# Own buffers and an earlier load for the background matrix-vector blocks of a two-layer trunk

## The chip, the cores and the metric

The kernel runs on one core of a Trainium2 chip. The metric is device time in microseconds (us) of one execution, the median of several runs. The kernel before takes 2971.46 us (three runs, 2971.45 to 2976.05). The core's engines are named as the profile names them: PE (TensorE, with PEld for its weight loads), DVE (VectorE), ACT (ScalarE), POOL (GpSimd) and SP (SyncE, which here only issues DMAs). Each engine takes its own list of instructions in order, and semaphores make it wait for others.

## The reference, cut to what matters

Two layers over 1024 tokens of width 1024, in float32. Each layer has a mixer (gated delta net in layer 0, retention in layer 1) and a convolutional feed-forward. Ahead of each of these the activations are scaled and shifted, and behind it they are gated, by vectors that depend on one conditioning vector `c`:

```python
def reference(x, c, cond_w, cond_b, ada_w, ada_b, ...):
    e = silu(c @ cond_w + cond_b)                       # 1024
    for i in range(2):
        mod = e @ ada_w[i] + ada_b[i]                   # 6 * 1024
        sh1, sc1, g1, sh2, sc2, g2 = split(mod, 6)
        y = mixers[i](x * (1 + sc1) + sh1)
        x = layer_norm(ALPHA * x + (1 + g1) * y, ...)
        y = conv_ffn(x * (1 + sc2) + sh2, ...)
        x = layer_norm(ALPHA * x + (1 + g2) * y, ...)
    return x
```

The product `e @ ada_w[i]` is a matrix-vector product with a 1024 x 6144 matrix. The change is about how ten of the twelve 1024-wide pieces of these products are computed; two of layer 0 are needed at once and are computed in the opening.

## The kernel before

TensorE works in a split float32: each operand is written as a high and a low part, and three matmuls replace one (`mm3`, `mma`). A weight unit is loaded raw into a buffer of tag `wr` (`load_w`, L100; the DMA is L102), ScalarE writes its high part `wh` (L89), VectorE its low part `wl` (L90). The tags `wr`, `wh` and `wl` have two buffers each.

The program runs through these stages: the opening (conditioning vector, the first scales and shifts, the first projections); layer 0's mixer, in which the chunk-by-chunk scan is interleaved with the projections that fill TensorE's gaps (`run`, `scan`, `filler`); its output projection; the first feed-forward, whose up projection is done by Strassen-like products (`strassen`, with one call of `wino` for each pair of weight units) and whose down projection is `proj_gen`; layer 1's projections, again in `strassen`; the retention core, interleaved with the value projections (`core`, `ret_v`, `ret_fill`); its output projection; and the second feed-forward.

A matrix-vector piece is background work. `bg_ada(i, j, kind)` (L205) puts eight functions into a list `bg`: two halves of 512 columns, four blocks each. A block is 256 rows by 512 columns, 512 KB. Its `unit` gets a buffer, issues the load on SP (L214) and returns the arithmetic, `work`: two operations on VectorE (L221, L223), each of which adds one row group, scaled by `e`, to a sum `ada`. There is one buffer of tag `ada`. With the fourth block of a half the sum over the partitions is finished: for a "col" piece by four transposes on TensorE, four accumulating operations on ScalarE (L235) and an addition on VectorE (L237 or L239); for a "row" piece by a matmul with ones (L245) and an addition (L246).

`bg_step` (L119) is called at fixed places of the main work: after each projection unit of the layer 0 mixer, twice in each `wino`, after each weight unit of the retention's value projection, and after each step of `proj_gen`. A call first issues the arithmetic that the last call left in `pend`, then takes the next function from `bg`. So a block's arithmetic is issued one call behind its load. The same list carries `bg_gain` (L377), which multiplies rows by a gain on POOL, with buffers of the tag `lane`.

The block's buffer comes from the ring named in `bg_tag`: `wr`, which the weight loads use as well, and inside `strassen` the ring `lane` (four buffers), which there also holds the two gate tiles `g` of the feed-forward, read by the convolution (L1564). The tag `xT` has four buffers of 128 x 512; the opening takes two of them, and nothing else uses them.

In all 80 blocks are loaded: 24 in the mixer of layer 0, 40 in the first feed-forward (its `strassen` has 40 calls), 8 in the retention core and 8 in the second feed-forward.

The order of the work on each engine is made before the run. TensorE's order in the two interleaved stages is written down by `run` with a clock of estimated latencies (`pq` pins it). All other orders are made by the framework's planner: it takes instructions by priority, earliest in the program first, when its own estimate of times says that their inputs and buffers are there, and it may take a later one when an earlier one isn't ready. On the chip the lists are then followed strictly.

```python
    BUFS = {..., "lane": 4, ..., "ada": 1, "wr": 2, "wh": 2, "wl": 2, ..., "xT": 4}
    ...
    def load_w(src, tags=("wh", "wl"), raw="wr", eng=dve):
        wr = tl(raw, [P, D])
        anchor["w"] = sp.dma_start(wr, src)
```

Of the kernel before, what the change touches and what calls it, by code (L numbers as in the profile page):

```python
# [15 lines left out]
P = 128  # L16
D = 1024
S = 1024
KT = D // P
HALF = 512  # L20
# [13 lines left out]
def trunk_kernel(ctx: ExitStack, tc, A):  # L34
    nc = tc.nc
    pe, act, dve, pool, sp = nc.tensor, nc.scalar, nc.vector, nc.gpsimd, nc.sync
# [4 lines left out]
    dr = ctx.enter_context(tc.tile_pool(name="dr", bufs=1, space=bass.MemoryType.DRAM))  # L41

    BUFS = {"hTa": 8, "hTb": 8, "qkv": 20, "aux": 4, "auh": 8, "lane": 4, "cv": 4, "ada": 1,
            "wr": 2, "wh": 2, "wl": 2, "t2": 3, "sm": 14, "sm2": 6, "st": 8, "s8": 6, "S": 4, "qx": 3, "fs": 1, "xT": 4}

    def tl(tag, shape, dt=F32, name=None):
        return sb.tile(shape, dt, tag=tag, name=name or tag, bufs=BUFS[tag])
# [7 lines left out]
    def ct(name, shape, dt=F32):  # L55
        return cp.tile(shape, dt, tag=name, name=name)
# [25 lines left out]
    def hs(half):  # L82
        return slice(half * HALF, (half + 1) * HALF)
# [30 lines left out]
    bg, pend = [], []  # L114

    bg_ps = [None]
    bg_tag = ["wr"]

    def bg_step(tile=mm_tile):  # L119
        bg_ps[0] = tile  # L120
        if pend:
            pend.pop()()
        if bg:
            nxt = bg.pop(0)()
            if nxt:
                pend.append(nxt)

    def gemm_feat(src, hT_, step=True):
        w = load_w(src)
        accs = [acc_tile() for _ in hT_]  # L130
        for a, ht in zip(accs, hT_):
            for k in range(KT):
                mm3(a, w, k, ht[k], k == 0, k == KT - 1)
        if step:
            bg_step(acc_tile)
        return accs
# [58 lines left out]
    def bias_cols(i, j):  # L195
        return ada_b[:, i * 48 + j * 8:i * 48 + j * 8 + 8]

    def row_load(src, key=None, eng=sp, tag="auh"):
        t = two(tag, F32, "rowb")
        with after(key):  # L200
            for hf in range(2):
                eng.dma_start(t[hf], src[:, hs(hf)].to_broadcast([P, HALF]))
        return t

    def bg_ada(i, j, kind):  # L205
        box = {}

        def unit(nh, kp):
            if kp == 0:
                box["a"] = tl("ada", [P, HALF])  # L210
            a = box["a"]
            wr = tl(bg_tag[0], [P, 2, HALF], name="mvw")
            c0 = j * D + nh * HALF
            sp.dma_start(wr, A["ada_w"][i, kp * 256:(kp + 1) * 256, c0:c0 + HALF].rearrange("(a p) n -> p a n", p=P))  # L214
            return lambda: work(nh, kp, a, wr)

        def work(nh, kp, a, wr):
            for kk in range(2):
                k = kp * 2 + kk
                if k == 0:  # L220
                    dve.tensor_scalar(a, wr[:, 0], e[:, 0:1], None, ALU.mult)  # L221
                else:
                    dve.scalar_tensor_tensor(a, wr[:, kk], e[:, k:k + 1], a, ALU.mult, ALU.add)  # L223
            if kp < KT // 2 - 1:
                return
            if kind == "col":
                if nh == 0:
                    vecs[i, j] = ct(f"v{i}{j}", [P, KT])
                gs = slice(4 * nh, 4 * nh + 4)
                v, b = vecs[i, j][:, gs], bias_cols(i, j)[:, gs]  # L230
                tp, pt = bg_ps[0](), tl("sm2", [P, 4], name="cs")
                for g in range(4):
                    pe.transpose(tp[:, g * P:(g + 1) * P], a[:, g * P:(g + 1) * P], ident)
                for g in range(4):
                    act.activation(a[:, g * P:(g + 1) * P], tp[:, g * P:(g + 1) * P], AF.Copy, accum_out=pt[:, g:g + 1])  # L235
                if j in (1, 2, 4):
                    dve.scalar_tensor_tensor(v, pt, 1.0, b, ALU.add, ALU.add)  # L237
                else:
                    dve.tensor_add(v, pt, b)  # L239
            else:  # L240
                if nh == 0:
                    rows[i, j] = row_load(A["ada_b"][i:i + 1, j * D:(j + 1) * D], ("x", i))
                g = rows[i, j][nh]
                pt = bg_ps[0]()
                pe.matmul(pt, ones, a, start=True, stop=True)  # L245
                dve.scalar_tensor_tensor(g, pt, 1.0, g, ALU.add, ALU.add)  # L246

        for nh in range(2):
            for kp in range(KT // 2):
                bg.append(lambda nh=nh, kp=kp: unit(nh, kp))  # L250
# [126 lines left out]
    def bg_gain(n, src, dst):  # L377
        gb = []

        def unit(c, r):  # L380
            if r == 0:
                gb[:] = [tl("auh", [P, HALF], name="gb") for _ in range(2)]
                for t, nm in zip(gb, ("ln_g", "ln_b")):
                    sp.dma_start(t, A[nm][n:n + 1, hs(c)].to_broadcast([P, HALF]))
            x = tl("lane", [P, HALF], name="xg")
            rs = slice(r * P, r * P + P)
            sp.dma_start(x, src[rs, hs(c)])
            if r == 7:
                return gain(x, rs, c)
            return lambda: gain(x, rs, c)  # L390

        def gain(x, rs, c):
            pool.tensor_tensor(x, x, gb[0], ALU.mult)
            pool.tensor_tensor(x, x, gb[1], ALU.add)
            sp.dma_start(dst[rs, hs(c)], x)

        for c in range(2):
            for r in range(8):
                bg.append(lambda c=c, r=r: unit(c, r))
# [139 lines left out]
    xT = {}  # L539
# [478 lines left out]
    def tail(p, h, q4):  # L1018
# [24 lines left out]
        elif all(("tail", g, 0) in events for g in pairs[p]):  # L1043
            give("lane", 1)
            emit(("M", p))

    bg_ada(0, 4, "col")
    bg_ada(0, 3, "col")
    bg_ada(0, 2, "col")
    kept = {}  # L1050
    zd = dr.tile([GH, P, S], F32, tag="zd", name="zd")
# [50 lines left out]
    c, z = "c", "z"  # L1102
# [54 lines left out]
    def strassen(hT0, xts, scale, shift, items, tags=("hTb", "hTb", "qkv", "qkv", "aux"), direct=False):  # L1157
# [86 lines left out]
            sink(2, prod(a22, "T4"), u3)  # L1244
            bg_step()

        bg_tag[0] = "lane"
        for n in range(2):
            if not direct:
                sinks[n] = items[n][2]()  # L1250
# [9 lines left out]
        for n in range(2, len(items)):  # L1260
            wino(n, items[n][2]())
            if items[n][3]:
                items[n][3]()
        bg_tag[0] = "wr"
        return B

    def ablk_of(src, tag="cv"):
# [247 lines left out]
    def layer_tail(i, mix, wout, xsrc, x_mid, x_out, ln_next, final):  # L1515
# [23 lines left out]
        def pair_items(fp):  # L1539
# [49 lines left out]
            return [(up[4 * fp], up[4 * fp + 2], gate_start, conv), (up[4 * fp + 1], up[4 * fp + 3], up_start, None)]  # L1589

        strassen(hT0, xts, sc2, sh2, [it for fp in range(NF // 2) for it in pair_items(fp)])
        slots = {"c": "hTa", "x": "qkv"}
        gb2 = gain_rows(3, ("mid", i), "hTb") if final else None
# [69 lines left out]
    def gate_item(u):  # L1663
        def start():
            def sink(q, a, b):
# [5 lines left out]

    sc_r, sh_r = next0()
    B = strassen(h0, xts, sc_r, sh_r, [gate_item(0), gate_item(2)]
                 + [rope_item(h, j) for h in range(RH) for j in range(2)] + [gate_item(u) for u in range(4, 16, 2)], ("hTa", "aux", "qkv", "qkv", "hTa"), True)
    hT = [h0, []]
    xlo = []
    for t in range(4):
        x = tl("cv", [P, 516], name="xlo")[:, 0:HALF]
# [270 lines left out]
```

## Time and profile before

| What | us |
|---|---|
| median of three runs | 2971.46 |
| span of the profiled execution | 2967.8 |
| the profiled execution's own time | not given beside its span |
| TensorE busy | 2820.5 (95%) |
| VectorE busy | 2242.4 (76%) |
| ScalarE busy | 1316.5 (44%) |

The span runs from the first to the last instruction of the profiled execution; the runs' times lie some 4 us above it. A row of the groups names the line, the engine, the operation, the tiles (out<-in), the shapes and the count, then busy time, the mean of one in ns, and the idle time of the engine just before it with what ended it. A row of the waits names who waited, for whom, and the total, the number of times and the longest. A row of the timeline has start, length, line, operation and, in brackets, the idle time before it. The chain is followed backwards from the last instruction of a stretch, at each step to what released it. "mvw" is the tile of a background block, `wr` a raw weight unit, `ada` the running sum.

### The profile page before, as it was taken

How to read it: one execution, taken by the hardware profiler on the slowest of the kernel's cores; microseconds unless marked ns; L12 is line 12 of the kernel's file. 1: busy time of each engine (PE TensorE's matmuls, PEld its weight loads, DVE VectorE, ACT ScalarE, POOL GpSimd, SP SyncE). 2: the span in 40 equal slices, each digit the busy share in tenths (PEclk: the TensorE clock that was granted, in tenths of full speed). 3: DMA queues.
4: the chain of work that ended last, by engine and by line, in shares of the span. 5: the costliest groups of instructions: out<-in, count | busy, mean ns of one | idle time of the engine just before them, and what ended most of it. 6: DMA issues, size and time to landing. Idle time of an engine off the chain costs nothing. (4 is left out here: it accounts for less than half of the span.)

```text
span 2967.8 us, 38939 instructions
## 1 busy us (share of the span) xinstructions
PE 2820.5 (95%) x13638; PEld 2304.5 (78%) x13638; DVE 2242.4 (76%) x4005; ACT 1316.5 (44%) x2413; POOL 474.8 (16%) x469
## 2 busy tenths in 40 slices
PE   8999898999999999999999999999999999999997
PEld 7887777887788888787877887777777788887786
DVE  5787787656688888879678645666689887777979
ACT  4744564444544444446433442222344544444443
POOL 0312221100001111610000202322202011112301
PEclk9999999999999999999999999999999999999998
DMA  7231222254245445865333544665664243335753
GB/s 275 79 113 65 86 79 79 83 167 160 91 158 163 158 151 174 305 198 179 120 128 117 181 160 152 203 189 175 205 212 157 91 135 107 107 107 176 274 183 137
DMA packets 244404, 451.01 MB, mean 152 GB/s; under 512 B 23088, under 2 KB 76592, under 8 KB 244208
## 3 DMA queue, kind: packets, MB, share of 16 engines
q1 hardware_dynamic: 213088, 401.07, 41.0%
q10 hardware_dynamic: 29760, 43.00, 4.0%
q0 software_dynamic: 1360, 4.46, 0.4%
q8 instruction: 107, 1.75, 0.3%
q14 instruction: 89, 0.73, 0.1%
HBM read 339.91 MB, written 108.53 MB: 151 GB/s over the span
## 5 line engine op out<-in xcount | busy, mean ns | idle before, releaser
L651 PE MATMUL acc<-hT,wh 128*128 128x512 f32 x960 | 299.3, 393 | 0.0
L1437 PE MATMUL acc<-bb,ab 128*128 128x512 f32 x984 | 231.4, 393 | 6.6 <-DVE bb L90 5.4
L1585 POOL TENSOR_TENSOR o<-o 128x512 f32<-128x512 f32 x80 | 110.7, 1394 | 716.4 <-DVE o L1578 490.8
L1437 PEld LDWEIGHTS acc<-bb,ab 128*128 128x128 f32 x984 | 182.6, 188 | 50.2 <-DVE bb L90 10.2
L1163 PE MATMUL acc<-T,wb 128*128 128x512 f32 x840 | 203.1, 391 | 6.7 <-DVE wb L90 6.7
L651 PEld LDWEIGHTS acc<-hT,wh 128*128 128x128 f32 x960 | 181.9, 190 | 34.1
L651 PE MATMUL acc<-hT,wl 128*128 128x512 f32 x480 | 201.1, 419 | 0.0
L89 ACT ACTIVATE ab<-ar 128x512 fp32r<-128x512 f32 x210 | 129.6, 625 | 152.7 <-PE mm L287 36.9
L90 DVE TENSOR_TENSOR ab<-ar,ab 128x512 fp32r<-128x512 f32 x210 | 161.9, 777 | 41.1 <-ACT ab L89 41.1
L1163 PEld LDWEIGHTS acc<-T,wb 128*128 128x128 f32 x840 | 157.0, 188 | 43.2 <-DVE wb L90 9.8
L90 DVE TENSOR_TENSOR wl<-wr,wh 128x1024 fp32r<-128x1024 f32 x95 | 119.7, 1260 | 69.6 <-ACT wh L89 68.6
L90 DVE TENSOR_TENSOR wb<-mm,wb 128x512 fp32r<-128x512 f32 x216 | 145.5, 682 | 31.2 <-ACT wb L89 30.6
L90 DVE TENSOR_TENSOR wb<-wr,wb 128x512 fp32r<-128x512 f32 x162 | 111.1, 691 | 69.8 <-ACT wb L89 69.1
L89 ACT ACTIVATE wh<-wr 128x1024 fp32r<-128x1024 f32 x95 | 100.7, 1061 | 132.3 <-PE acc L651 53.1
L1224 ACT ACTIVATE pc<-acc 128x512 f32<-128x512 f32 x143 | 84.9, 593 | 160.7 <-PE acc L1163 97.4
L1564 DVE SCALAR_TENSOR_TENSOR o<-g,vc,o 128x512 f32<-128x512 f32 (+2 forms) x176 | 145.4, 843 | 4.7 <-ACT o L1559 4.1
L89 ACT ACTIVATE wb<-mm 128x512 fp32r<-128x512 f32 x216 | 124.0, 595 | 51.9 <-DVE mm L1213 50.3
L89 ACT ACTIVATE wb<-wr 128x512 fp32r<-128x512 f32 x162 | 99.4, 628 | 104.0 <-DMA wr<-in_ffn_up 38.8
L651 PE MATMUL acc<-wh,hT 128*128 128x512 f32 x384 | 135.6, 415 | 1.6 <-DVE vv L90 1.6
L110 PE MATMUL acc<-T,wb 128*128 128x512 f32 x292 | 116.0, 397 | 9.4 <-DVE wb L90 9.4
L472 DVE SCALAR_TENSOR_TENSOR qkv<-raw,vc,qkv 128x512 f32<-128x512 f32 x144 | 111.6, 779 | 11.5 <-ACT qkv L470 10.7
L223 DVE SCALAR_TENSOR_TENSOR ada<-mvw,e,ada 128x512 f32<-128x512 f32 x140 | 106.9, 764 | 17.4 <-DMA mvw<-in_ada_w 17.1
(641 smaller groups left out, 7466.8 us busy)
## 6 DMA issues: line engine op xcount, KB each, us to landing
wr<-in_ffn_up SPq DMA_DIRECT2D x92, 512.0 KB, 4.4
mvw<-in_ada_w SPq DMA_DIRECT2D x80, 512.0 KB, 4.3
ad<-o SPq DMA_DIRECT2D x154, 256.0 KB, 3.1
ar<-ad SPq DMA_DIRECT2D x154, 256.0 KB, 3.9
Br<-in_ffn_down SPq DMA_DIRECT2D x88, 256.0 KB, 3.8
wr<-in_ret_wv SPq DMA_DIRECT2D x32, 512.0 KB, 3.9
ar<-od SPq DMA_DIRECT2D x56, 256.0 KB, 5.3
xs<-xt ACTq DMA_DIRECT2D x24, 512.0 KB, 3.7
```

The source lines that it names most:

```text
L89: act.activation(dst_h, src, AF.Copy)
L90: eng.tensor_tensor(dst_l, src, dst_h, ALU.subtract)
L110: mm(acc, wl[:, k], hl[0], start=first, stop=False)
L223: dve.scalar_tensor_tensor(a, wr[:, kk], e[:, k:k + 1], a, ALU.mult, ALU.add)
L472: dve.scalar_tensor_tensor(oh, raw[:, 3 - j:515 - j], w[:, 3 - j:4 - j], oh, ALU.mult, ALU.add)
L651: pq(pe.matmul(out, lhsT, rhs, start=start, stop=stop), cost)
L1163: return pe.matmul(*a, skip_group_check=True, **kw)
L1224: act.activation(t, X, AF.Copy)
L1437: return pe.matmul(*args, skip_group_check=True, **kw)
L1564: dve.scalar_tensor_tensor(tv, gv[:, c0 - j:c1 - j], w[:, 2 - j:3 - j], tv, ALU.mult, ALU.add)
L1585: (dve if fp == 0 else pool).tensor_tensor(o[d], o[x], o[y], op)
```

## The change

The blocks get buffers of their own: the tag `xT` now has two buffers, each large enough for a block (128 x 2 x 512), in the same space as the four small ones. `bg_tag` goes. A function in `bg` now returns, with its arithmetic, how many calls later that is to be issued: 2 for a block, 1 for a gain. `bg_step` counts these down, in order; once `bg` is empty it issues one left-over arithmetic per call. The sum buffer `ada` is taken at a half's first arithmetic and no longer at its first load.

```diff
-            ..., "fs": 1, "xT": 4}
+            ..., "fs": 1, "xT": 2}
...
-    bg_tag = ["wr"]
...
-        if pend:
-            pend.pop()()
+        for p in pend:
+            p[0] -= 1
+        while pend and (pend[0][0] <= 0 or not bg):
+            pend.pop(0)[1]()
+            if not bg:
+                break
         if bg:
             nxt = bg.pop(0)()
             if nxt:
-                pend.append(nxt)
+                pend.append(list(nxt))
...
         def unit(nh, kp):
+            wr = tl("xT", [P, 2, HALF], name="mvw")
+            c0 = j * D + nh * HALF
+            sp.dma_start(wr, A["ada_w"][i, kp * 256:(kp + 1) * 256, c0:c0 + HALF].rearrange("(a p) n -> p a n", p=P))
+            return 2, lambda: work(nh, kp, wr)
+
+        def work(nh, kp, wr):
             if kp == 0:
                 box["a"] = tl("ada", [P, HALF])
             a = box["a"]
-            wr = tl(bg_tag[0], [P, 2, HALF], name="mvw")
-            c0 = j * D + nh * HALF
-            sp.dma_start(wr, A["ada_w"][i, kp * 256:(kp + 1) * 256, c0:c0 + HALF].rearrange("(a p) n -> p a n", p=P))
-            return lambda: work(nh, kp, a, wr)
-
-        def work(nh, kp, a, wr):
             for kk in range(2):
...
-            return lambda: gain(x, rs, c)
+            return 1, lambda: gain(x, rs, c)
...
-        bg_tag[0] = "lane"
...
-        bg_tag[0] = "wr"
```

More of the change, by code (lines that the diff above doesn't have):

```diff
@@ L43, in trunk_kernel @@
     BUFS = {"hTa": 8, "hTb": 8, "qkv": 20, "aux": 4, "auh": 8, "lane": 4, "cv": 4, "ada": 1,
-            "wr": 2, "wh": 2, "wl": 2, "t2": 3, "sm": 14, "sm2": 6, "st": 8, "s8": 6, "S": 4, "qx": 3, "fs": 1, "xT": 4}
+            "wr": 2, "wh": 2, "wl": 2, "t2": 3, "sm": 14, "sm2": 6, "st": 8, "s8": 6, "S": 4, "qx": 3, "fs": 1, "xT": 2}
     def tl(tag, shape, dt=F32, name=None):
```

## The prediction

> **What bounds the kernel now.** I read the page first, then busy time by stretch, then who waited for whom inside each stretch, then the chain of work that ended last in the one stretch where background blocks are waited for.
>
> ```profile
> span 2967.8 us, 38939 instructions
> PE 2820.5 (95%) x13638; PEld 2304.5 (78%) x13638; DVE 2242.4 (76%) x4005; ACT 1316.5 (44%) x2413; POOL 474.8 (16%) x469
> L223 DVE SCALAR_TENSOR_TENSOR ada<-mvw,e,ada 128x512 f32<-128x512 f32 x140 | 106.9, 764 | 17.4 <-DMA mvw<-in_ada_w 17.1
> ```
> ```profile
> 200.00:560.00 360.00, 331.26 (x2329) 282.02 (x2328) 287.03 (x773) 198.51 (x441) 81.07 (x125) 0.95 0.26 85
> 830.00:1190.00 360.00, 359.60 (x1595) 296.29 (x1594) 310.24 (x485) 173.46 (x339) 50.27 (x36) 1.00 0.48 156
> 1190.00:1230.00 40.00, 33.00 (x137) 25.89 (x136) 34.11 (x42) 16.92 (x38) 26.05 (x17) 0.96 0.92 338
> 1930.00:2030.00 100.00, 92.11 (x402) 68.95 (x400) 64.11 (x119) 20.20 (x34) 20.29 (x28) 0.98 0.62 187
> ```
>
> TensorE bounds it: 95% of the span, so a change helps only where TensorE stands idle. In the second fence each row is a stretch, its length, busy time of PE, PEld, DVE, ACT and POOL, the granted clock, the DMA share and GB/s. The background blocks run in four places: 24 of them under the scan of layer 0 (first row, 28.7 us of idle TensorE), 40 in the first feed-forward (second row, 0.4 us idle), 8 in the retention core (last row, 7.9 us idle), 8 in the second feed-forward. The profiled execution has a span of 2967.8 us; no separate time is given for it, and the median of the runs, 2971.46, is 3.7 us above the span. I add the sum to the median one for one, as the change touches neither end of the program.
>
> ```profile
> PE sc L651 <- DVE Sr L1752: 3.5, 1, 3.5
> PE sc L651 <- DVE on L1780: 1.3, 2, 1.0
> PE acc L651 <- DVE wl L90: 1.0, 2, 0.8
> PE mm L654 <- DVE on L1780: 0.8, 1, 0.8
> PE acc L651 <- DVE vv L90: 0.6, 1, 0.6
> ```
> ```profile
>   DMA mvw<-in_ada_w: 13.6, 6
> ```
> ```profile
> 1951.11 3.82 DMA op<-od
> ...
> 1966.91 4.77 DMA mvw<-in_ada_w
> ...
> 1972.38 1.22 DVE wl L90
> ...
> 1974.26 0.61 DVE Sr L1752
> 1974.91 1.15 PE sc L651 x3
> ...
> 2013.99 4.47 DMA mvw<-in_ada_w
> ```
>
> These are TensorE's waits in 1930:2030 (all five, 7.2 us in total), the idle time of engines before work on mvw in 1900:2060 (13.6 us in six waits), and the chain of 1930:2030. The chain shows how they hang together: VectorE takes its instructions in order, stands before a background block until its load lands (1966.91 + 4.77), then does a weight split, the rest of the block, and only at 1974.26 the state copy Sr for which TensorE waits 3.5 us.
>
> **The change part by part.**
>
> *Loads two calls ahead, retention core.* The block's arithmetic no longer follows its load. If the six waits go, all 7.2 us of TensorE's waits may go. With them goes a slow stretch:
>
> ```profile
> 1968.52 1.52 PE L651 MATMUL sc<-vv,kz 128*128 128x512 f32 x6
> ...
> 1975.86 0.63 PE L651 MATMUL acc<-wh,22_13012 128*128 128x512 f32 x1
> ...
> 1978.85 0.45 PE L651 MATMUL acc<-wl,22_13012 128*128 128x512 f32 x1
> ...
> 1979.37 0.39 PE L651 MATMUL acc<-wh,22_13032 128*128 128x512 f32 x1
> 1979.59 0.40 PE L651 MATMUL acc<-wl,22_13032 128*128 128x512 f32 x1
> ```
>
> Seven matmuls start between 1975.86 and 1978.85, 0.43 us apart; at 1979.37 it is 0.22. Lost: 2.99 - 7 x 0.23 = 1.4 us. Sum for this stage: 7.2 + 1.4 = 8.6 us. Upper bound: the two transfers on the chain, 4.77 + 4.47 = 9.2 us. Lower bound 0: the chain has other transfers of that length ready to be late next (op<-od, 3.82 us), and with two buffers the third and fourth block of each half are still loaded only when the first two are used up, so up to half of the six waits can come back. I take 8.6, as the row nearest to the end, Sr, waits on nothing else late: TensorE's products that it copies (1968.52, six of them) were issued well before the idle time.
>
> *Own buffers, layer 0.* A block no longer takes one of the two wr buffers, so weight loads stop waiting for blocks:
>
> ```profile
> SPq L102 <- DVE ada L223: 52.6, 6, 22.9
> ACT wh L89 <- DMA wr<-in_gdn_wqkv: 14.5, 4, 5.0
> DVE v L239 <- ACT ada L235: 4.0, 1, 4.0
> PE mm L651 <- DVE qkv L928: 6.0, 3, 2.5
> PE mm L654 <- DVE DT L963: 5.8, 3, 2.5
> ```
>
> In 200:560 the SP queue stood 52.6 us before weight loads until blocks were done, and ScalarE 14.5 us before weights that came late. But no row of TensorE in that stretch names a weight; what it waits for are the scan's own operations (the last two rows are two of ten such groups). The double-buffered wh and wl cover the lateness; without that cover it would cost at most the 14.5 us. A gain bound for the stage is the two groups that have background work ahead of them on VectorE, 6.0 + 5.8 = 11.8 us. The same operations remain, in another place, so it can also lose: a block left in front of a scan operation, as the one at 326.00 here, costs up to the 2.49 us of TensorE's wait at 327.48.
>
> ```profile
> 322.68 0.16 DVE L239 TENSOR_TENSOR v<-cs,vc 128x4 f32<-128x4 f32 x1 [4.03 <-ACT ada L235]
> ...
> 326.00 0.74 DVE L223 SCALAR_TENSOR_TENSOR ada<-mvw,e,ada 128x512 f32<-128x512 f32 x1
> ```
> ```profile
> 327.48 1.75 PE L651 MATMUL mm<-T,U 32*32 32x32 f32 x30 [2.49 <-DVE qkv L928]
> ```
>
> Between +11.8 and a loss of several such waits (the slower rival) I take 0: the nearest rows say that weights are not what TensorE waits for, and the scan's order is not edited.
>
> *Own buffers, feed-forward.* Blocks leave the lane ring, so their loads no longer wait for the gate convolution:
>
> ```profile
> SPq L214 <- DVE o L1564: 54.3, 12, 5.5
> ```
> ```profile
> PE acc L1163 <- DVE wb L90: 0.3, 1, 0.3
> ```
>
> 54.3 us of the SP queue, with the next weight loads and block stores behind it; but TensorE waits 0.3 us in 830:1190 (second row, its only wait there). Worth 0; TensorE's own work, 359.6 of 360 us, covers it. The cost, had that cover been gone, would be at most the 54.3. The 8 blocks of the second feed-forward are the same case.
>
> *One call later at the end.* The first feed-forward has 40 calls for 40 blocks, so two blocks, not one, are worked after it, where VectorE splits the first operands of the down projection:
>
> ```profile
> PE acc L285 <- DVE ab L90: 7.0, 4, 2.8
> ```
>
> VectorE is busy 34.11 of the 40 us of 1190:1230 and TensorE waits 7.0 us for it. One more block is two operations of 0.764 us: 1.5 us, charged in full. Bounds: 0 (it may be done in an earlier gap) and 3.0 (both blocks in front of the split).
>
> *No cost.* The sum buffer is taken at the first arithmetic rather than at the load; that only unties the load. The opening uses two of the four small xT tiles, and two large tiles take the same space. Row gains keep their lag of one call. No instruction or DMA is added: 80 loads and their 160 operations stay. On SP, loads pass other issues; each issue takes under half a microsecond. SP can stand before a block's load only until the block two earlier is used.
>
> **Sum:** -7.2 - 1.4 + 0 + 0 + 1.5 = -7.1 us, so 2971.46 - 7.1 = 2964.4 us, 0.24% faster; a measurement of this kernel can tell about 0.2%, 5.9 us.
>
> **The rivals.**
>
> *Hidden anyway.* The six waits go but the retention chain is set by the next transfer: op<-od (3.82 us) and its like lead to the same TensorE operations. For it: the chain goes through them several times already. Against: the 3.5 us wait names the state copy, which no such transfer feeds. The time is 2971 (within 2967 to 2975).
>
> *Layer 0 gains too.* With weights early and blocks already landed, both groups behind background work shrink: 11.8 us more, so 2964.4 - 11.8 = 2952.6; half of it gives 2958. For it: the wait of 4.03 us at 322.68 stands directly ahead of the scan. Against: that wait is for ScalarE's sums, which stay.
>
> *Slower: background work lands in the scan.* What a call issues is not run in the order written: each engine's list is made ahead of time from planned times.
>
> ```profile
> L202 SPq DMA_DIRECT2D rowb<-in_ada_b x6: 346/400/428, 670.0 to 2033.5; - x6
> L246 DVE SCALAR_TENSOR_TENSOR rowb<-mm,rowb x6: 678/692/692, 861.4 to 2436.9; 128x512 f32<-128x512 f32 x6
> ```
>
> The last row load went out at 2033.5 and was used at 2436.9, 400 us later. Blocks with buffers of their own, always landed, can be planned into any short gap of VectorE, and where the gap is not there they push the scan back. Place: 200:560; price 2.49 us each. Three cancel the gain (7.1 / 2.5), six more than now make it slower by over 0.2%; eight of the 24 blocks give -7.1 + 20 = +13 us, 2984. Against: the present plan has 24 blocks there too and two or three such waits.
>
> [...]
>
> ```profile
> 1214.31 0.78 PE L285 MATMUL acc<-bb,ab 128*128 128x512 f32 x1 [2.51 <-DVE ab L90]
> 1214.88 0.63 PE L286 MATMUL acc<-bb,ab 128*128 128x512 f32 x1
> ```
>
> By these rows a collision can cost 2.5 + 1.4 = 3.9 us, and eight would give 2995; I keep 2.5, since most waits in the scan are shorter.
>
> *Slower: early loads in front of weight loads.* A block's 512 KB sent just ahead of a weight load holds it up. Landing of weight loads in layer 0:
>
> ```profile
> DMA to landing us min/median/max: 3.3/3.5/6.0
> ```
>
> The worst lies 2.7 us over the least. The five or so loads there that are already awaited would cost 5 x 2.7 = 13.5 us, so 2978; it decides where ScalarE has no slack. Against: those loads are the ones that the change frees.
>
> [...]
>
> **How the numbers follow.** The forecast holds with 0.42 (2960 to 2969; 0.31 of it below 2965.5, 0.11 within 0.2%). Layer 0 gains too: 0.13, faster. Hidden anyway: 0.17, same. Scan collisions: 0.22, slower. Loads in the way: 0.06, slower. So faster 0.31 + 0.13 = 0.44, same 0.11 + 0.17 = 0.28, slower 0.22 + 0.06 = 0.28. The range runs from the second rival's end to the middle of the collisions: 2953 to 2982.
>
> **What would show it.** After: in the retention core mvw waits fall from 13.6 us to under 4, no mvw transfer on that chain, TensorE's waits there from 7.2 to about 1 us; no weight load that waits for a block, and none of 54.3 us behind the convolution; TensorE's idle time in the scan within 3 us of 28.7; its wait at the down projection 8 to 9 us. The prediction is wrong if the scan's idle time grows by more than 7 us, or if the state copy is late for another reason.

## The result and the profile after

The changed kernel takes 2978.15 us (median of 20 runs, 2969.25 to 2988.46), beside 2971.45 us for the kernel before in the same sessions (20 runs, 2964.29 to 2976.05). The ratio is 1.0023, with a 95% interval of 1.0013 to 1.0032: slower by 6.7 us, where 2964.4 and a gain of 7.1 had been forecast. The profiled execution after has a span of 2979.7 us and a time of 2981.43, 3 us above the median. In every execution measured the time lies 1.7 to 2.4 us above the span (not some 4), so the execution of before with its span of 2967.8 took about 2970, somewhat below its median. The two spans differ by 11.9 us, more than the medians do.

First the page of the kernel after, then its busy time by stretch (columns as in the prediction):

```profile
span 2979.7 us, 38997 instructions
PE 2832.3 (95%) x13638; PEld 2312.3 (78%) x13638; DVE 2246.2 (75%) x4005; ACT 1320.0 (44%) x2415; POOL 461.1 (15%) x469
```
```profile
200.00:560.00 360.00, 327.51 (x2287) 277.85 (x2286) 278.98 (x765) 192.28 (x428) 72.44 (x114) 0.94 0.24 80
830.00:1190.00 360.00, 356.14 (x1572) 292.17 (x1573) 303.14 (x474) 169.19 (x333) 50.75 (x36) 1.00 0.47 157
1190.00:1230.00 40.00, 35.34 (x147) 27.78 (x146) 33.11 (x47) 18.79 (x39) 11.40 (x9) 0.96 0.70 243
1930.00:2030.00 100.00, 98.49 (x447) 75.68 (x447) 61.97 (x117) 22.45 (x37) 17.88 (x26) 1.00 0.51 158
```

The retention core (last row) did what was forecast: TensorE's idle time there falls from 7.9 to 1.5 us. But the scan (first row) idles 32.5 us instead of 28.7, and the first feed-forward (second row) 3.9 instead of 0.4, and each of these wins or losses is carried on to the end. Where the time goes is clearest when the same matmul of TensorE is looked up in both traces and its start after is set against its start before (median over the matmuls of the 25 us from there on; worked out from the two traces, us):

```
start before        175   300   350   600   800   825  1150  1275  1900  2050  2325  2375  2900
after - before     -0.7  -0.6   4.9  10.2  10.5  12.0  15.3  16.8  16.3   6.1  11.3  13.0  13.8
```

So the scan loses about 11 us in this pair of executions, the first feed-forward 6.3 (800 to 1275), the retention core gains 10.2, and about 5 are lost between it and the second feed-forward, another 1.7 at that one's start. The 5 are no effect of the change: two kernels below that keep the old ring everywhere (with most block arithmetic left out in one stage) lose 5.2 and 5.3 there too, so the execution of before was quick in that stretch. One trace is one execution, and a stage's loss read from a single pair carries such differences.

**What the planner made of it.** The loads and the work of some blocks, from the two traces (start of the load, start of the first operation on it, us):

```
block                               before             after
first of first feed-forward      793.5   813.2     531.0   818.2
second of first feed-forward     824.5   834.5     533.4   823.7
first of retention piece        1929.4  1933.7    1200.1  1502.6
fifth (second half)             1974.3  2009.0    1510.3  2027.8
first of second feed-forward    2328.5  2348.2    2039.3  2354.1
```

With buffers that nothing else uses, a block is loaded as soon as the block two earlier is used up, in whatever stage that is: the first blocks of the retention piece are loaded at the end of the first feed-forward, and its first half is worked during layer 1's projections, 400 us ahead of its calls; the second half's first two blocks are loaded right behind that, but worked in the retention core as before. These are that tile's rows in 1400:2100:

```profile
L226 DVE SCALAR_TENSOR_TENSOR ada<-mvw,e,ada x14: 740/746/1295, 1503.6 to 2042.3; 128x512 f32<-128x512 f32 x14
L214 SPq DMA_DIRECT2D mvw<-in_ada_w x8: 372/376/379, 1504.4 to 2043.1; - x8
DMA to landing us min/median/max: 3.7/4.5/7.7
```

Columns: line, engine, operation, tiles, count, duration least/median/most in ns, first and last start. Nothing idles for mvw there (13.6 us before), and TensorE's waits in 1930:2030 fall from 7.2 to 1.5 us:

```profile
PE sc L654 <- DVE on L1781: 1.3, 1, 1.3
PE mm L657 <- DVE on L1781: 0.2, 1, 0.2
```

In the scan the work mostly moves later, not earlier. The last three halves of its pieces begin on VectorE at 323.4, 416.7 and 492.2 us before and at 342.6, 437.7 and 521.9 after.

The price is paid elsewhere. In the first feed-forward it shows in the weight splits wb. The first Strassen product waits for one in both kernels, 4.69 us before and 4.89 after, mostly behind convolution operations. The next wait is the one that grows. These are TensorE's two waits there, before and then after, and VectorE ahead of the second one, after:

```profile
813.37 0.79 PE L110 MATMUL acc<-T,wb 128*128 128x512 f32 x1 [4.69 <-DVE wb L90]
819.34 2.83 PE L1163 MATMUL acc<-T,wb 128*128 128x512 f32 x11 [0.63 <-DVE wb L90]
```
```profile
823.86 0.79 PE L110 MATMUL acc<-T,wb 128*128 128x512 f32 x1 [4.89 <-DVE wb L90]
831.42 2.78 PE L1166 MATMUL acc<-T,wb 128*128 128x512 f32 x11 [2.08 <-DVE wb L90]
```
```profile
823.12 0.68 DVE L90 TENSOR_TENSOR wb<-mm,wb 128x512 fp32r<-128x512 f32 x1
823.72 0.74 DVE L226 SCALAR_TENSOR_TENSOR ada<-mvw,e,ada 128x512 f32<-128x512 f32 x1
...
827.57 0.74 DVE L226 SCALAR_TENSOR_TENSOR ada<-mvw,e,ada 128x512 f32<-128x512 f32 x1
...
830.03 0.74 DVE L226 SCALAR_TENSOR_TENSOR ada<-mvw,e,ada 128x512 f32<-128x512 f32 x1
830.69 1.28 DVE L90 TENSOR_TENSOR wb<-mm,wb 128x512 fp32r<-128x512 f32 x2
```
```profile
PE acc L1166 <- DVE wb L90: 4.3, 4, 2.1
```

Three block operations stand between two rounds of splits; before there are two (0.48 and 0.74 us, at 813.23 and 816.74). From one round to the next it is 7.6 us after and 6.0 before. The last line is TensorE's only group of waits in 830:1190: 4.3 us, where it was 0.3. In the steady state the four blocks of a half are worked within 16 us after (1110 to 1126, for instance) and 22 before (1096 to 1118).

### The profile page after: what moved, and what is told of

The parts are those of the page before. It is cut to its first block, busy times and chain, and to the rows that moved or that the text cites. A ratio compares the mean times of both kernels' runs of the same rounds, so it can differ in the third digit from the quotient of the medians.

```text
span 2979.7 us, 38997 instructions
## 1 busy us (share of the span) xinstructions
PE 2832.3 (95%) x13638; PEld 2312.3 (78%) x13638; DVE 2246.2 (75%) x4005; ACT 1320.0 (44%) x2415; POOL 461.1 (15%) x469
## 5 line engine op out<-in xcount | busy, mean ns | idle before, releaser
L90 DVE TENSOR_TENSOR wb<-mm,wb 128x512 fp32r<-128x512 f32 x216 | 145.0, 682 | 28.7 <-ACT wb L89 27.9
L89 ACT ACTIVATE bb<-Bw 128x512 fp32r<-128x512 f32 x120 | 74.0, 624 | 105.6 <-DVE Bw L1312 27.1
```

The lines of the kernel that those rows point to most:

```text
L89: act.activation(dst_h, src, AF.Copy)
L90: eng.tensor_tensor(dst_l, src, dst_h, ALU.subtract)
```

## The experiments

Each kernel was timed against the kernel before on the same chip. "Own" means that the named pieces take the two `xT` buffers, and all others the old rings (`wr`, in `strassen` `lane`) with a lag of one call. The edit common to these kernels:

```diff
+    bg_tag = ["wr"]
+    OWN = {(1, 2)}          # retention piece; other kernels: other sets
...
+            own = (i, j) in OWN
+            if not own and kp == 0:
+                box["a"] = tl("ada", [P, HALF])
-            wr = tl("xT", [P, 2, HALF], name="mvw")
+            wr = tl("xT" if own else bg_tag[0], [P, 2, HALF], name="mvw")
...
-            return 2, lambda: work(nh, kp, wr)
+            return 2 if own else 1, lambda: work(nh, kp, wr)
```

### One stage at a time

Retention piece alone:

> Only the eight blocks of the retention core's piece have the two xT buffers and the lag of two calls; all others keep the wr or lane ring, the lag of one call and the sum buffer taken at the load. Theory A (each stage has its own effect: the ring of their own lets the planner place blocks early and in bunches; retention gains, scan and feed-forward lose): the retention core keeps its gain of about 9 us and nothing else moves, so about 2962 us, ratio 0.997. Theory B (the lag of two calls is what costs): about the same gain here, 2962. Theory C (any re-planning shifts the time by a few us, no stage is to blame): anywhere in 2966 to 2978.

The scan's 24 blocks alone, `OWN = {(0, 4), (0, 3), (0, 2)}`:

> Only the 24 blocks under the scan of layer 0 have the xT buffers and the lag of two. Theory A: the loss of the scan alone, some 9 us by the profile after, so about 2980, ratio 1.003, with the added TensorE idle time between 320 and 620 us. Theory B: the same. Theory C: 2966 to 2978, and the scan's idle time within 3 us of before.

The feed-forwards' 48 blocks alone, `OWN = {(0, 5), (1, 1), (1, 0), (1, 4), (1, 3), (1, 5)}`:

> Only the 40 blocks of the first feed-forward and the 8 of the second have the xT buffers and the lag of two. Theory A: bunches of four blocks delay weight-block splits by 0.3 to 1.5 us per pair of units, some 6 to 8 us in all, so about 2978, ratio 1.002, with TensorE waiting some 4 us for wb in 830 to 1195 us. Theory B: as A. Theory C: 2966 to 2978 and those waits under 1 us.

All pieces own, `return 1` instead of `return 2`:

> All blocks have the xT buffers, but their arithmetic is issued one call behind the load, as before. Theory A: what matters is the ring of their own, so the time stays near that of the change, 2976 to 2980, with blocks still worked in bunches. Theory B: without the second call the loss goes and the gain of the retention core stays, about 2963. Theory C: anywhere in 2966 to 2980.

| kernel | us | ratio | 95% interval |
|---|---|---|---|
| before (25 runs) | 2970.68 | | |
| retention own | 2961.16 | 0.9971 | 0.9960 to 0.9982 |
| scan own | 2977.44 | 1.0026 | 1.0014 to 1.0037 |
| feed-forwards own | 2978.91 | 1.0029 | 1.0018 to 1.0040 |
| all own, lag of one call | 2974.80 | 1.0011 | 1.0000 to 1.0022 |

The stages add up: -9.5 + 6.8 + 8.2 = +5.5 us, beside the 6.7 measured for the whole change. So the retention core alone is faster than both kernels, and two stages take the gain back, as theory A had it. With a lag of one call the change still gains nothing; 2974.80 lies between what theories A and B expected there, so the second call can be a part of the loss.

In the scan block arithmetic comes onto the path. This is the chain of 325:365 in the kernel with the scan's blocks own; first its shares by line, then some pieces (start, length, engine, tile, line):

```profile
by line: PE acc L659 30.5%; PE mm L659 30.2%; issue 8.2%; DVE ada L231 5.9%; DVE jk L799 3.9%; DVE qkv L480 3.5%; PE mm L662 2.8%; DVE R L924 2.8%; DVE U L945 2.3%; PE sc L659 2.2%; ACT qkv L478 1.8%; ACT xb L914 1.5%; ACT qkv L995 1.4%; DV
...
346.10 0.41 DVE R L924
346.50 0.96 DVE ada L231
347.46 0.67 DVE R L924 x2
...
350.37 0.67 DVE ada L231
351.04 0.08 DVE sk L802
351.12 0.32 DVE U L945
351.43 0.18 issue
351.62 0.74 DVE ada L231
```

Three block operations stand between R and U, on which the scan's next matmuls hang: 5.9% of 40 us, 2.4 us. TensorE's operations of the scan are unchanged.

This is one place, not the whole loss. The execution shown took 2968.11 us, the least of that kernel's twelve, and TensorE's idle time in 200:560 is 29.7 us in it, where the kernel before has 28.7: the idle time that theory A expected is not there. Worked out from the traces as above, this is how much longer than before the same matmuls took, for the kernel with the scan own and for three others of this section (us):

```
stretch (time before)       200-300  300-325  325-365  365-500  500-620
scan own                        1.1     -3.4      2.7     -1.5      4.4
the same, most left out        -3.7     -3.4     -1.5     -1.3      3.5
old ring, most left out         0.8     -2.4      0.0     -0.9      4.8
all own, lag of one call       -2.2     -0.2      2.0     -0.7     -0.2
```

What 325:365 loses, the stretch ahead of it had gained, and what is lost behind 500 is lost without most of the arithmetic too. Over 200 to 620 kernels with an unchanged scan differ from before by -0.5 to +2.9 us, so single traces do not show where the 6.8 us of the medians are.

In the feed-forward the bound itself changes. The chain of 830:1250, by line, with the feed-forwards' blocks own, and then with them in the lane ring (the kernel named "lag of one" below):

```profile
by line: PE acc L1171 13.1%; DMA wr<-in_ffn_up 8.6%; DVE o L1572 8.3%; DVE wb L90 7.4%; PE sc L1171 6.6%; DVE mm L1221 6.4%; issue 5.9%; DVE ada L231 3.8%; PE acc L112 3.5%; PE acc L110 3.5%; PE acc L111 3.5%; DVE g L1558 2.7%; ACT wb L89 2
```
```profile
by line: PE acc L1171 22.7%; PE sc L1171 11.2%; PE acc L112 9.9%; PE acc L111 9.9%; PE acc L110 9.9%; PE sc L112 4.8%; PE sc L111 4.8%; PE sc L110 4.7%; PE acc L293 1.6%; PE acc L294 1.5%; PE acc L295 1.5%; DVE o L1572 1.4%; DMA ar<-ad 1.4%
```

With the old ring the chain is TensorE nearly all the way (the eight largest entries alone make 77.9%). With the own ring much of it runs over VectorE, ScalarE and the weight loads, and 3.8% of 420 us, 16 us, is block arithmetic. By the same matmuls this kernel loses 3.4 us at 800 to 850 (the waits shown above), 5.0 at 950 to 1190 and 4.5 at the start of the second feed-forward (2340 to 2400).

### Ring or lag

Retention piece own, with a lag of one call (`return 1`):

> Only the retention core's piece has the buffers of its own, and its arithmetic follows its load by one call as before the change, not by two. Theory A (the ring of its own is what helps: with it the planner loads and works blocks far ahead of the program, and the number of calls between matters little): 2961 to 2963, as with two calls. Rival (two calls are needed): the six waits come back in part, 2965 to 2970.

2959.29 us (2958.64 to 2959.69), ratio 0.9958 (0.9946 to 0.9970): the fastest kernel here, and it needs no second call. TensorE's waits in 1900:2060:

```profile
PE sc L659 <- DVE on L1788: 2.6, 2, 1.5
PE mm L662 <- DVE on L1788: 0.3, 2, 0.2
```

The other way round, a lag of two in the feed-forwards without a ring of its own:

```diff
+            late = bg_tag[0] == "lane"
             wr = tl(bg_tag[0], [P, 2, HALF], name="mvw")
...
-            return 1, lambda: work(nh, kp, wr)
+            return 2 if late else 1, lambda: work(nh, kp, wr, late)
```

> The lag of two without the ring of its own, in the feed-forwards alone: blocks stay in the lane ring of four, the arithmetic follows the load by two calls, and the sum buffer is taken at the first arithmetic. Theory A (the ring of its own, free to be filled at any time, is what lets the blocks run ahead): within 2 us of the kernel before, 2969 to 2973, with blocks spread as before. Theory B (the lag of two itself costs): 2977 to 2979 as with the own ring.

2971.47 us, ratio 0.9996 (0.9987 to 1.0005), no change. So in the retention core and in the feed-forwards the ring does it, for better and for worse, and not the lag. For the scan neither run says it. With all blocks own and a lag of one call its last three halves begin at 320.2, 414.5 and 489.2 us, where they were before, and in that one trace the scan is 1.3 us shorter (the sum of the last row of the first table above); whether ring or lag costs there stays open.

### Arithmetic or the rest of the plan

The same kernels with most block arithmetic left out, in the own ring and in the old one:

```diff
             for kk in range(2):
                 k = kp * 2 + kk
-                if k == 0:
+                if (i, j) in SK and kp < 3:
+                    continue
+                if k == (6 if (i, j) in SK else 0):
                     dve.tensor_scalar(a, wr[:, 0], e[:, 0:1], None, ALU.mult)
```

> Only the scan's 24 blocks have the buffers of their own and the lag of two. Left out: the multiplications of the first three blocks of each half, so that only the last block of a half is multiplied (the sums there are not the reference's); all loads stay. That takes 18 of 24 blocks' arithmetic, 36 operations of 0.76 us, from VectorE. Theory S1 (block arithmetic in front of the scan's operations is the loss): 2971 or less, and TensorE's idle time in 200:560 falls below that of before, 28.7 us. Theory S2 (the re-planned rest, weights, splits and table loads, is the loss): it stays at 2975 to 2978 with nearly no block arithmetic there.

> The control for the run before that left out block arithmetic in the scan: buffers and lag as before the change for every block, and the multiplications of the first three blocks of each half are left out in the scan's 24 blocks (the sums there are not the reference's). Theory S1 (what the own buffers cost in the scan is block arithmetic placed in front of scan operations): the old and the new ring come out alike once the arithmetic is gone, 2964 to 2969 as with the own ring (2966.7). Theory S2 (the re-planned weights and table loads cost the 7 us whatever the blocks do): this kernel is about 7 us faster than the one with the own ring, near 2960.

> The feed-forwards' 48 blocks have the buffers of their own and the lag of two; scan and retention core are as before. Left out: the multiplications of the first three blocks of each half of these 48 (the sums there are not the reference's); all loads stay. Theory A1 (the arithmetic, worked early and in bursts in front of the weight splits, is what costs): 2969 to 2972, and no wait of TensorE for wb over 0.5 us in 830:1190. Theory A2 (the loads, which go out in another order, are what costs): 2976 to 2979.

> The control: the same multiplications of the feed-forwards' blocks left out, with buffers and lag as before the change. As TensorE was busy for 359.6 of 360 us in the first feed-forward, all theories expect no more than 1 or 2 us of gain over the kernel before, 2969 to 2972; a larger gain says that block arithmetic cost something there before the change already.

| ratio to the kernel before | old ring | own ring |
|---|---|---|
| scan, all arithmetic | 1 | 1.0026 (1.0014 to 1.0037) |
| scan, most left out | 0.9985 (0.9974 to 0.9996) | 0.9979 (0.9969 to 0.9990) |
| feed-forwards, all arithmetic | 1 | 1.0029 (1.0018 to 1.0040) |
| feed-forwards, most left out | 1.0005 (0.9995 to 1.0014) | 1.0007 (0.9998 to 1.0016) |

Without the arithmetic the two rings are alike in both stages (2968.23 and 2966.67 us in the scan, 2973.20 and 2974.15 in the feed-forwards), within about 4 us by the intervals; with it the own ring costs 7 to 8 us. So the loads in their new order, the freed weight loads and the shifted table loads (20 on ScalarE before and 22 after, 1.28 us each) do not make the loss by themselves, up to that uncertainty; the loss needs the block arithmetic, and it is not there with the same arithmetic in the old ring. Two expectations were missed. In the scan TensorE's idle time in 200:560 is 32.2 us with the arithmetic left out, and theory S1 had it below 28.7; and 2974.15 us in the feed-forwards lies between the two theories' ranges. In the feed-forward TensorE is again busy for all of 830:1190 and waits for nothing:

```profile
830.00:1190.00 360.00, 360.00 (x1593) 297.12 (x1593) 275.86 (x429) 174.91 (x341) 50.26 (x36) 1.00 0.46 153
```

VectorE's busy time there falls from 310 to 276 us. That the 86% that it was busy before left no room fits this, but no run varies it by itself. At the ends of this stretch the execution shown, the longest of its kernel's twelve, still loses. Again by the same matmuls (us longer than before):

```
stretch (time before)          800-850  850-950  950-1190  1190-1230  2340-2400
feed-forwards own                  3.4     -0.9       5.0        0.2        4.5
the same, most left out            3.5     -1.0       0.0        6.0        0.0
old ring, most left out           -1.1     -1.0       0.2        2.2       -0.6
own, three wr buffers              1.8     -0.9       4.4        4.4        3.3
```

Kernels with unchanged feed-forwards stay within 0.2 us in the first, third and last of these stretches. So the block arithmetic is the loss at 950 to 1190 and at the start of the second feed-forward. At the start of the first one, and where the down projection's first operands are split (11.1 us of TensorE's waits in 1185:1260, where it is 7.0 before and 8.6 with the old ring and the same arithmetic left out), the own ring still costs without it in this execution; why, the runs don't show.

### Placing the work differently

Here the blocks keep the own ring, and their arithmetic is forbidden to come ahead of the last weight split or convolution operation written before its call (retention piece own in both):

```diff
-            for kk in range(2):
+            with after("d" if (i, j) in HELD else None):
+              for kk in range(2):
```

> The blocks of the two feed-forwards and of the retention core have the buffers of their own and the lag of two; the scan's blocks are as before. In the feed-forwards a block's arithmetic may not be placed ahead of the last weight split or gate convolution written before its call, so it can no longer be worked far ahead of the program and in bursts of four; no instruction is added or removed. Theory A1 (the feed-forward loses because blocks that lie ready are worked in bursts of four, about 12 us, in front of the weight splits): the waits of TensorE for wb in 830:1190 go back from 4.3 us to under 1, and the time is that of the retention piece alone, 2961 to 2963. Theory A2 (the loss is in the loads, which no longer wait for the gate convolution and go out in front of weight loads): the waits stay and the time is 2969 to 2971 (2961 and the 8 us that the feed-forward pieces cost by themselves).

> The scan's blocks and the retention piece have the buffers of their own and the lag of two; the feed-forwards' blocks are as before. In the scan a block's arithmetic may not be placed ahead of the last weight split or convolution on VectorE written before its call. Theory S1 (the scan loses because a block that lies ready is worked in front of the scan's operations): close to 2961 to 2963, the time of the retention piece alone. Theory S2 (the loss comes from the rest of the plan, which shifts since weight loads no longer wait for blocks: weights, splits, ScalarE's table loads): 2967 to 2969, that time and the 7 us that the scan's blocks cost by themselves.

2979.30 us (1.0026, 1.0015 to 1.0037) and 2980.60 us (1.0032, 1.0018 to 1.0046). Neither theory of either pair had this. The hold made new waits: of the feed-forward's kernel these are TensorE's largest in 830:1190 and in 1190:1250, of the scan's kernel its largest in 200:620.

```profile
PE sc L112 <- DVE wb L90: 4.0, 2, 2.5
...
PE acc L297 <- DVE ab L90: 13.6, 3, 12.4
```
```profile
PE acc L245 <- DVE ada L235: 17.0, 3, 7.4
```

Held blocks come late: in front of the direct products' splits, of the down projection's first operands (12.4 us at once), and in the scan TensorE stands before the transposes that finish a sum. These two runs don't tell the theories apart; they do show that placing alone can cost 7 to 10 us: the single stages add to -1.3 us for the one and -2.7 for the other, and +6.2 and +7.5 were measured.

A ring of one own buffer, lag of one, lets no four landed blocks be worked together:

> The feed-forwards' 48 blocks in a ring of their own as in the change, but of one buffer, and with a lag of one call, so that a block can be loaded only when the one before it is used up, and the four of a half can't be worked back to back. Scan and retention core as before. Theory A1 in its narrow form (what costs is four landed blocks worked in one burst in front of the weight splits): 2970 to 2973, and the chain of the first feed-forward is TensorE's again. Theory A in its wide form (any ring of its own costs there, since blocks are no longer held back by the lane buffers that the convolution uses): 2976 to 2979, and the chain still goes through VectorE and the loads of the up projection's weights.

> The same for the scan's 24 blocks alone: one buffer of their own, lag of one call; the rest as before. Weight loads still never wait for a block. Theory S1 in its narrow form (bursts of landed blocks in front of scan operations): 2970 to 2973 or a little faster. Wide form (any ring of its own lets blocks be placed where they hurt): 2975 to 2978.

2993.18 us (1.0071, 1.0058 to 1.0085) in the feed-forwards, slower than either form of the theory had it, and 2976.73 us (1.0015, 1.0006 to 1.0024) in the scan, as the wide form had it. Taking the bursts away does not take the loss away. Nor does it show that bursts cost nothing, as this ring brings a wait of its own: in the feed-forward VectorE now stands before landing blocks, in 830:1190:

```profile
  DMA mvw<-in_ada_w: 12.1, 18
```

Last, a third buffer in the weight ring (`"wr": 3`), to see whether late weight loads carry the loss:

> The feed-forwards' blocks in the ring of two buffers of their own with the lag of two, as in the run that cost 8 us, and the weight ring wr with three buffers instead of two. Theory L (block arithmetic delays VectorE's last read of a raw weight unit, so its buffer comes free late, the next weight load goes out late, and VectorE and ScalarE then wait for it, a loop through the two wr buffers): the third buffer cuts the loop, the chain of the first feed-forward is TensorE's again, and the 8 us go: at most 2972. Without the loop (the blocks simply stand in front of splits that TensorE waits for): it stays above 2976, with the chain through VectorE.

> The control and perhaps the better version: the retention piece alone in buffers of its own, lag of one, and the weight ring with three buffers. What the third buffer is worth by itself, with the feed-forward's blocks in the lane ring: in the feed-forward nothing, as TensorE is the chain there; in the scan it frees the weight loads from the blocks. All theories: 2955 to 2961; a slower time says that the freed weight loads alone re-plan the scan for the worse.

> The whole change with three wr buffers. Theory L: the feed-forward's 8 us go, the scan's 7 us stay, the retention core's gain stays: 2966 to 2971, as against 2978. Without the loop: 2976 to 2980.

| kernel with three wr buffers | us | ratio | two buffers |
|---|---|---|---|
| feed-forwards own | 2974.83 | 1.0009 (1.0000 to 1.0018) | 1.0029 |
| retention own, lag of one | 2964.08 | 0.9970 (0.9960 to 0.9981) | 0.9958 |
| whole change | 2977.24 | 1.0016 (1.0003 to 1.0030) | 1.0023 |

Idle time of engines before work on wr in 830:1190, before, after, and with the feed-forwards own and three buffers:

```profile
  DMA wr<-in_ffn_up: 27.5, 23
```
```profile
  DMA wr<-in_ffn_up: 44.6, 21
```
```profile
  DMA wr<-in_ffn_up: 28.2, 18
```

The third buffer takes the late weight loads back to where they were, and the feed-forward kernel comes out 5 us closer to before, though the intervals touch. But TensorE's waits for wb stay at 2.9 us there, the same matmuls at 950 to 1190 still lose 4.4 us of 5.0 (last row above), the 2972 that the loop theory allowed at most is missed, and the whole change gains nothing that the intervals show. So late weight loads are a part of the feed-forward's loss at most; for the rest the traces show block work directly in front of splits. How the loss divides between the two stays open. The third buffer shows no gain by itself either: 2964.08 us is above the 2955 to 2961 that all theories expected, and the retention kernel is rather slower with it, though the intervals overlap.

## Why the prediction was wrong

- *Loads two calls ahead, retention core, -8.6 us.* Right in sign and about in size: -9.5 us with a lag of two, -13.8 with a lag of one (their intervals overlap). The six waits went and no other transfer took their place, so the rival "hidden anyway" falls. The mechanism was half right: not the second call, but a ring that nothing else uses; half of the blocks were worked in another stage altogether.
- *Own buffers, layer 0, "I take 0".* This step failed: +6.8 us (scan alone). The prediction looked at what TensorE waited for before and found no weights, and that was right, but the own ring, with its lag of two, moved 1.5 us of VectorE work per block to other places (up to 30 us later) of a stage in which TensorE waits for VectorE's scan operations in many small steps (18 waits in 200:560 before, 20.6 us in all, the longest 2.5). With most of that arithmetic left out the loss is gone; at which waits it arises, and whether ring or lag moves it, stays open. The slower rival had named the place and the kind of collision: 6.8 / 2.49 is 2.7 such waits, and three were said to cancel the gain. That its price fits is not shown: in the trace of the whole change the scan takes 10.9 us longer, and TensorE's idle time grows by only 3.8. It was given 0.22.
- *Own buffers, feed-forward, "worth 0; TensorE's own work, 359.6 of 360 us, covers it".* This step failed too, by +8.2 us, within the intervals as much as the scan. TensorE's full busy time said that a faster supply could gain nothing. It was read as saying also that a worse supply would cost nothing. In its place the runs show block operations between the weight splits: TensorE's waits for wb in 830:1190 grow from 0.3 to 4.3 us, and both they and the 5.0 us at 950 to 1190 are gone with most of the arithmetic left out. The row beside it, VectorE at 310 of 360 us, could have warned how thin that cover was. The 8 blocks of the second feed-forward, "the same case", lose at its start in the same way (4.5 us in the trace). No rival had a loss in the feed-forward.
- *"No cost": SP can stand before a block's load until the block two earlier is used.* True and dear to look at. SP's waits in 830:1190 after:

```profile
SPq L214 <- DVE ada L226: 123.3, 34, 5.2
...
SPq L1222 <- DVE mm L1216: 30.2, 18, 14.0
```

  SP stands 123.3 us before block loads, with the next weight loads behind them. Yet it still waits for VectorE in 18 of 19 weight loads, so mostly it is there in time, and the kernel with most arithmetic left out, whose SP stands as long (127.2 us), loses nothing at 950 to 1190. Costing this at nothing holds for that stretch; for the two ends of the feed-forward the runs don't separate it. Not every issue takes under half a microsecond, either: those of the 80 block loads before took 0.38 us in the median and 1.11 at most.
- *One call later at the end, +1.5 us.* TensorE's idle time in 1190:1230 was to grow by that; it is 4.7 us after, 7.0 before. But this stretch holds other work after, as the program runs some 16 us later there. Followed by the same matmuls, 1190 to 1275 takes 0.2 us longer, so the 1.5 us were not paid in this pair of executions.
- *Loads in front of weight loads* (the rival with 0.06): the left-out arithmetic speaks against it, since all loads stayed in those kernels. The 6.0 us landing that it was priced from is that of the weight load issued at 331.08, 2.4 us behind a block's (328.69). That this rival's time, 2978, is the measured one is luck.

The sum by measured terms is -9.5 + 6.8 + 8.2 = +5.5, where it was -8.6 + 0 + 0 + 1.5. Of the signs named, the retention core's came true (mvw waits 13.6 to 0, TensorE's waits 7.2 to 1.5), and so did those of the loads (weight loads wait 0.4 us for blocks in 200:560 instead of 52.6, block loads no longer for the convolution): these waits went, and nothing was won by it. The down projection's wait for ab was to be 8 to 9 us; it is 5.4 after, beside 7.0 before. Two rows told of the loss: TensorE's idle time in the scan, 3.8 us up where 3 was the limit (the 7 that the prediction took as a sign of being wrong were not reached), and the 0.3 us of wb that became 4.3, for which the prediction had set no mark.

## What to carry to other kernels

A full engine is a ceiling for gains, not a cushion against losses (TensorE was busy 359.6 of 360 us in the first feed-forward, and the feed-forwards' own ring cost 8.2 us): before a step is costed at zero because TensorE is busy, look at how busy the engine is that feeds it and what its next operation in line is. Buffers shared with other work also pace background work (block loads waited 54.3 us for the convolution in 830:1190 before, and not at all after); a ring of its own sets the planner free to place that work elsewhere, here 400 us early for half of the retention piece, which helped where the work had been late, and between the weight splits of the feed-forward, where it hurt. So give the ring only to the stage that waits (here the retention piece alone, 2959.3 us, 0.42% faster than before), and change one stage at a time.

## What was not expected of the hardware

The same order of work can take 6 us more in one stretch through TensorE's clock alone. Stretch 325:365 of the kernel with the scan own, and of the whole change, whose matmuls have the same order in 310:365 and whose waits of TensorE there are the same to 0.1 us (the longest 1.9):

```profile
325.00:365.00 40.00, 36.50 (x359) 30.75 (x357) 30.50 (x91) 21.41 (x40) 9.74 (x12) 0.91 0.37 120
```
```profile
325.00:365.00 40.00, 36.46 (x298) 30.04 (x296) 26.38 (x71) 16.57 (x28) 9.53 (x10) 0.75 0.36 120
```

The granted clock is 0.91 and 0.75; 0.16 of 40 us is 6.4 us, and TensorE gets through 298 matmuls instead of 359. The starts of the same matmuls differ by 6.2 us more behind this stretch than ahead of it. That is a large part of why the scan's loss is larger in the profile of the whole change than the 6.8 us of the medians. It needs no change to the scan either: the kernel with the one-buffer ring in the feed-forwards has the TensorE order of the kernel before in all 13638 matmuls, and around this stretch (318:368) the same three groups of waits as before, yet its granted clock in 320:365 is 0.81 where it is 0.92 before, and the same matmuls (325 to 365) take 4.2 us longer. What sets the granted clock the runs don't show. The length of a single wait does not settle it: in the trace of before, the next seven matmuls start 0.22 to 0.33 us apart behind a wait of 2.82 us (1208.76) and 0.42 to 0.57 apart behind one of 2.51 (1214.31).
